# A decoder layer on one core: the down projection by seven block products, with h's operands kept in DRAM

## The chip, the core and the metric

The kernel runs on one core of one Trainium2 chip. The metric is the device time of one execution in microseconds (us), smaller is better. Of the kernel before, three runs took 2142.36, 2143.44 and 2143.82 us; the median is 2143.44 us. The profiled execution that all rows below come from took 2143.53 us, and its span, from the first to the last instruction, is 2141.7 us.

## The reference

One decoder layer works on 512 tokens of width 2048, in float32:

```python
hn   = rms_norm(x, norm_mix_pre);  proj = hn @ w_in          # 2048 -> 6144
a    = diff_attention(q, k, v, ...);  c = gate_b * short_conv(gate_c * hc, conv_w)
x    = x + rms_norm(concat(a, c) @ w_out, norm_mix_post)
hn   = rms_norm(x, norm_ffn_pre)
f    = (silu(hn @ w_gate) * (hn @ w_up)) @ w_down            # 2048 -> 5632 -> 2048
out  = x + rms_norm(f, norm_ffn_post)
```

The change is in the last two matrix stages: gate/up (two matrices of 2048 x 5632) and down (5632 x 2048). Below, h is the 512 x 5632 matrix silu(gate) * up.

## The kernel before

**Number format.** A float32 operand is split into a high part and a rest, both in TensorE's reduced float32 type: `split` (L95 to L97) has ScalarE (ACT) cast the high part (L96) and VectorE (DVE) subtract it from the source for the low part (L97). One product of two tiles is then three matmuls, high x high, high x low and low x high, issued by `mm3` (L118 to L121). So nearly all matmuls of the kernel have line L119, L120 or L121, and nearly all casts and subtractions L96 and L97.

**Gate and up.** The 5632 columns of w_gate and w_up are taken 256 at a time, gate and up by turns, as 44 *quartets* (the 2 x 2 blocks of such a piece of weights). A quartet is computed with seven block products instead of eight, by a Strassen-Winograd scheme: `combine` (L770) forms sums and differences of weight blocks on DVE, `prepare` (L784) splits the operand of one product into one of four ring tiles, `product` (L806) issues its 8 x 3 matmuls of 256 columns, and `gather` (L823) puts the products together in SBUF. Operands of the activations (`ffn_hi`, `ffn_lo` in `acts`, and the places x0 to x5) are made once, before this stage. `gate_up` (L865) issues the products in the order of the list `order` (L738) and prepares operands three products ahead. `finish` (L852) multiplies silu(gate) by up; the first 4 of h's 44 chunks of 128 rows stay in SBUF, the other 40 go to DRAM as `hd` (L863).

**Down.** 5632 is 44 chunks of 128. The chunks are taken in 5 groups of 4, 12, 12, 12 and 4 (`first_kc`, L900). For the group in work, h's chunks are read back from `hd` (`load_h`, L902), split, and kept. Weights come 4 chunks x 512 columns at a time, 1 MB, with rows of 2 KB (`down_spec`, L918), are split into two ring tiles each (`load_chunk`, L106), and used for four token tiles of 128: `down_part` (L922) issues 4 x 3 matmuls of 512 columns, with h's tile stationary and the weights moving. When a group's last chunk is in, `add_down` (L928) adds the bank to the sum in SBUF. The last group (`down_last`, L953) also adds up squares, normalizes, adds the residual read back from `x1d` and stores the result.

**What sets the order.** The program is written as jobs (`run_jobs`, L156); a tile scheduler then places instructions on each engine and adds the waits. Each engine works through its list in order; the DMAs of this part are all issued by SyncE's queue (SP), in order as well. A pool of SBUF tiles that is closed and replaced by another makes the first writers of the new tiles wait for the last users of the old ones.

Of the kernel before, what the change touches and what calls it, by code (L numbers as in the profile page):

```python
# [11 lines left out]
F32 = mybir.dt.float32  # L12
# [6 lines left out]
P = 128  # L19
# [13 lines left out]
SUB_EPS = 1e-5  # L33
LAMBDA_INIT = 0.8 - 0.6 * math.exp(-0.3 * 0)
# [19 lines left out]
def trunk(ctx: ExitStack, tc: tile.TileContext, a, out):  # L54
# [511 lines left out]
    hd = dram.tile([FF // P, P, S], F32, name="hd")  # L566


    def place(tag, dtype=F32, shape=(P, D)):
        count = late["count"] = late.get("count", 0) + 1  # L570
        name = f"{tag}_{count}"
        return late["fp"].tile(list(shape), dtype, tag=tag, bufs=1, name=name)

    def open_ffn(_):
        late["fp"] = ctx.enter_context(tc.tile_pool(name="ffn", bufs=1))
        late["mix"] = [place(f"m{t}") for t in range(NT)]
# [162 lines left out]
    raws, heads_raw, operands, psq, tmp, slots, hts = {}, {}, {}, {}, {}, {}, {}  # L739
# [44 lines left out]
    def prepare(n):  # L784

        q, i = order[n]
        if i in (1, 2) and 0 < q < HEAD:
            src = heads_raw[q][:, 8 * (i - 1) : 8 * i, :]
        else:
            (p11, p21), (p12, p22) = ((r[:, :, :P], r[:, :, P:]) for r in raws[q])  # L790
            src = {1: p11, 2: p12, 3: p12, 4: p22, 5: tmp.get("s1"), 6: p21, 7: p21}[i]
            if i in (3, 6):
                combine(q, {3: 4, 6: 2}[i])
        w = ring_tile(16, P, f"w_{q}_{i}").rearrange("p (a k) m -> p a k m", a=2)
        split(w[:, 0], w[:, 1], src)
        operands[n] = w

    def moving(i, part, k):
# [5 lines left out]
        return late[{6: 2, 7: 3, 4: 4}[i]][part].rearrange("p (t k n) -> p t k n", t=2, n=P)[:, :, k, :]  # L804

    def product(n):  # L806
        q, i = order[n]
        if i == 1:
            psq[q] = {"a": mm_bank(f"pa_{q}")}
        pq = psq[q]  # L810
        if i == 5:
            pq["b"] = aux_bank(f"pb_{q}")
        if i == 6:
            pq["d"] = (mm_bank if q else aux_bank)(f"pd_{q}")
        if i == 3:
            pq["c"] = aux_bank(f"pc_{q}")
        bank, half = {1: "a0", 2: "a1", 5: "b0", 7: "b1", 3: "c0", 4: "c1", 6: "d0"}[i]
        o = pq[bank][:, 256 * int(half) :][:, :256]
        w = operands.pop(n)
        for k in range(8):  # L820
            mm3(o, w[:, 0, k, :], w[:, 1, k, :], moving(i, 0, k), moving(i, 1, k), k == 0, k == 7)

    def gather(n):  # L823
# [3 lines left out]
        if i == (5 if early else 1):  # L827
            tmp["q1", q] = slot("q1")
            nc.scalar.copy(tmp["q1", q], pq["a"][:, :256])  # L829
            if not up:  # L830
                tmp["sg", c] = slot("sg")
            tmp["r", q] = slot("r") if up else tmp["sg", c]
        if i == 7:
# [3 lines left out]
        if i == 6:  # L837
            u = tmp["u", q] = slot("u")
            nc.vector.tensor_add(u, pq["d"][:, :256], tmp["q1", q])
            nc.vector.tensor_add(tmp["r", q][:, 768:], tmp["r", q][:, 768:], u)  # L840
        if i == (6 if early else 2):
            nc.vector.tensor_add(tmp["r", q][:, :256], pq["a"][:, 256:], tmp["q1", q])
        if i != 4:
            return
        u, r, sg = tmp["u", q], tmp["r", q], tmp["sg", c]
        nc.vector.tensor_add(r[:, 256:768], pq["c"], tmp["q57", q])
        mid = r[:, 256:768].rearrange("p (h n) -> p h n", h=2)
        nc.vector.tensor_tensor(out=mid, in0=mid, in1=u[:, None, :].broadcast_to([P, 2, 256]), op=ALU.add)
        if not up:
            nc.scalar.activation(sg, sg, AF.Silu)  # L850

    def finish(q):  # L852
# [3 lines left out]
        sg, r = tmp["sg", c], tmp["r", q]  # L856
        nc.vector.tensor_mul(sg, sg, r)
        if c < 2:
            if c == 0:
                hts[0] = [tuple(place(t, F32R, (P, 4, S)) for t in ("spare", "m3"))]  # L860
            split(*(x_[:, 2 * c : 2 * c + 2, :].rearrange("p k n -> p (k n)") for x_ in hts[0][0]), sg)
# [158 lines left out]
```

## Time and profile before

| what | value |
|---|---|
| median of three runs | 2143.44 us |
| profiled execution, its span | 2143.53 us, 2141.7 us |
| TensorE (PE) busy | 2110.2 us, 99% of the span |
| weight loads (PEld), beside PE | 1886.7 us, 88% |
| DVE busy | 1308.1 us, 61% |
| ACT busy | 809.3 us, 38% |
| gate/up, from its first product to down's first | 785.2 to 1651.7 us |
| down without the last group | 1651.7 to 2088.6 us |
| last group, norm and store | 2088.6 to 2141.7 us |

Busy shares are means over stages that differ: DVE is busy 84% of a stretch of gate/up and a third of one of down. Matmuls overlap each other, so the time between the starts of two matmuls, not the duration of one, tells what a matmul costs. "Idle before" in a group of instructions is idle time of that engine just ahead of them, and the releaser is what ended it.

### The profile page before, as it was taken

The page shows a single profiled execution, that of the slowest core. Times are in us where ns is not written, and L with a number is a line of the kernel's source. Part 1 is how long each engine was busy: PE and PEld are TensorE (multiplying, and loading weights), DVE is VectorE, ACT ScalarE, POOL GpSimd, SP SyncE. Part 2 cuts the span into 40 slices and gives each one's busy share as a digit, 9 for nine tenths or more (in the row PEclk, how much of TensorE's full clock was granted, in tenths as well). Part 3 has the DMA queues.
Part 4 walks back from the last instruction along what each step waited for, and adds up shares of the span by engine and source line. Part 5 has one row for each costly group of instructions (what it writes and reads, how often), then busy time and mean ns, then how long its engine had stood idle before and what let it go on. Part 6 is the DMA issues. An engine that isn't in the chain of part 4 may idle for free.

```text
span 2141.7 us, 30431 instructions
## 1 busy us (share of the span) xinstructions
PE 2110.2 (99%) x13118; PEld 1886.7 (88%) x13118; DVE 1308.1 (61%) x1635; ACT 809.3 (38%) x1065; POOL 30.2 (1%) x51
## 2 busy tenths in 40 slices
PE   7999999999999998999999999999999999999998
PEld 6888888888888888999999999999999888888886
DVE  5226355463752389988888888888887532422336
ACT  4234243443532265544444444444444321211122
POOL 0000000000000010000000000000000000000000
PEclk9999999999999999999999999999999999999999
DMA  7322322222234343333333343333433532423233
GB/s 246 113 99 89 99 84 86 97 89 99 79 138 137 138 171 119 125 120 128 129 125 103 128 138 128 110 119 129 138 109 133 216 125 97 157 99 118 98 118 118
DMA packets 197831, 261.74 MB, mean 122 GB/s; under 512 B 9368, under 2 KB 146584, under 8 KB 195264
## 3 DMA queue, kind: packets, MB, share of 16 engines
q1 hardware_dynamic: 196384, 255.05, 35.0%
q10 hardware_dynamic: 1312, 4.74, 0.7%
q8 instruction: 103, 1.69, 0.3%
q14 instruction: 32, 0.26, 0.0%
HBM read 240.88 MB, written 21.52 MB: 123 GB/s over the span
## 4 chain that ended last, share of the span: by engine, by line
PE 94%; DVE 4%; DMA 1%; issue 0%; ACT 0%; POOL 0%; SPq 0%; DVEq 0%; POOLq 0%; ACTq 0%
PE pd L121 9%; PE pd L120 9%; PE pd L119 9%; PE pa L119 4%; PE pc L121 3%; PE pc L119 3%; PE pc L120 3%; PE pb L121 3%; PE pb L119 3%; PE pb L120 3%; PE pa L120 3%; PE pa L121 3%; PE po L119 3%; PE po L120 3%; PE po L121 3%; PE pc_h L119 1%
## 5 line engine op out<-in xcount | busy, mean ns | idle before, releaser
L97 DVE TENSOR_TENSOR lo_d<-raw_d,hi_d 128x2048 fp32r<-128x2048 f32 x42 | 96.2, 2291 | 185.5 <-ACT hi_d L96 185.5
L119 PE MATMUL pa<-acts,w 128*128 128x256 f32 x704 | 199.1, 283 | 1.1 <-ACT w L96 0.8
L121 PE MATMUL pa<-acts,w 128*128 128x256 f32 x704 | 194.8, 277 | 0.3 <-DVE w L97 0.3
L120 PE MATMUL pa<-acts,w 128*128 128x256 f32 x704 | 195.0, 277 | 0.0
L96 ACT CAST w<-raw_q 128x1024 fp32r<-128x1024 f32 x130 | 136.5, 1051 | 134.8 <-PE pc L121 33.5
L96 ACT CAST hi_d<-raw_d 128x2048 fp32r<-128x2048 f32 x42 | 80.0, 1906 | 277.5 <-PE pd L121 262.6
L97 DVE TENSOR_TENSOR w<-raw_q,w 128x1024 fp32r<-128x1024 f32 x130 | 156.8, 1221 | 13.7 <-ACT w L96 13.7
L119 PE MATMUL pd<-hi_d,acts 128*128 128x512 f32 x384 | 149.4, 389 | 0.0
L121 PE MATMUL pd<-hi_d,acts 128*128 128x512 f32 x384 | 149.4, 389 | 0.0
L120 PE MATMUL pd<-lo_d,acts 128*128 128x512 f32 x384 | 149.4, 389 | 0.0
L119 PEld LDWEIGHTS pa<-acts,w 128*128 128x128 f32 x704 | 132.2, 188 | 9.2 <-ACT m L829 8.2
L121 PEld LDWEIGHTS pa<-acts,w 128*128 128x128 f32 x704 | 132.2, 188 | 0.5 <-DVE w L97 0.5
L120 PEld LDWEIGHTS pa<-acts,w 128*128 128x128 f32 x704 | 132.2, 188 | 0.0
L121 PE MATMUL pb<-acts,w 128*128 128x256 f32 x352 | 98.1, 279 | 3.0 <-DVE w L97 3.0
L119 PE MATMUL pd<-x,w 128*128 128x256 f32 x352 | 98.0, 278 | 1.7 <-ACT w L96 1.7
L121 PE MATMUL pd<-x,w 128*128 128x256 f32 x352 | 98.3, 279 | 1.3 <-DVE w L97 1.3
L119 PE MATMUL pb<-acts,w 128*128 128x256 f32 x352 | 97.9, 278 | 0.1
L120 PE MATMUL pd<-x,w 128*128 128x256 f32 x352 | 97.9, 278 | 0.0
L121 PE MATMUL pc<-acts,w 128*128 128x256 f32 x352 | 97.3, 276 | 0.5 <-DVE w L97 0.5
L120 PE MATMUL pb<-acts,w 128*128 128x256 f32 x352 | 97.8, 278 | 0.0
L119 PE MATMUL pc<-acts,w 128*128 128x256 f32 x352 | 97.2, 276 | 0.0
L120 PE MATMUL pc<-acts,w 128*128 128x256 f32 x352 | 97.2, 276 | 0.0
(283 smaller groups left out, 6122.6 us busy)
## 6 DMA issues: line engine op xcount, KB each, us to landing
raw_q<-in_w_gate SPq DMA_DIRECT2D x44, 1024.0 KB, 5.1
raw_d<-in_w_down SPq DMA_DIRECT2D x44, 1024.0 KB, 5.0
post<-in_w_up SPq DMA_DIRECT2D x22, 1024.0 KB, 5.1
pre<-in_w_up SPq DMA_DIRECT2D x22, 1024.0 KB, 5.4
raw_o<-in_w_out SPq DMA_DIRECT2D x16, 1024.0 KB, 5.0
hd<-m SPq DMA_DIRECT2D x20, 512.0 KB, 2.8
raw_h<-hd SPq DMA_DIRECT2D x10, 1024.0 KB, 5.1
raw_v<-in_w_in SPq DMA_DIRECT2D x8, 1024.0 KB, 6.7
```

The costliest lines, as they stand in the source:

```text
L96: nc.scalar.copy(hi, src)
L97: nc.vector.tensor_tensor(out=lo, in0=src, in1=hi.bitcast(F32), op=ALU.subtract)
L119: nc.tensor.matmul(o, lhsT=lhi, rhs=rhi, start=start, stop=False)
L120: nc.tensor.matmul(o, lhsT=lhi, rhs=rlo, start=False, stop=False)
L121: nc.tensor.matmul(o, lhsT=llo, rhs=rhi, start=False, stop=stop)
```

## The change

`quartets`, products and rings of gate/up stay. New is that

- of the 22 pieces of h (256 rows, two chunks each), 20 (`NP`) go through the down projection by seven block products: a pair of chunks x two halves of the tokens is a 2 x 2 block of h, and the pair x two halves of 512 columns is a 2 x 2 block of w_down. The last two pieces (4 chunks) go as before, in `down_last`;
- `finish` makes the four sums and differences of h's blocks on DVE, and the high and low parts of all seven operands; `store_h` writes them to DRAM (`hx`, 7 operands x 20 pairs, high and low; `hl` for the last 4 chunks);
- the 20 pairs are taken in three groups of 7, 7 and 6 (`FIRST`). `load_slot` reads one operand of a group, high and low, both token halves, in four DMAs, into the place of gate/up's (or the former group's) operand of the same product, as soon as that product has been computed for the last time;
- weights come as blocks of 7 (or 6) chunks x 256 columns, 1 KB rows (`load_block`); DVE forms the four differences; each product is done in two halves of 4 and 3 (or 3 and 3) pairs, called steps: 3 groups x 4 column blocks x 7 products x 2 halves = 168 steps, each with 24 or 18 matmuls of 256 columns;
- products that enter the same sums are accumulated in one bank, in down and in gate/up too: there, product 2 is added to product 1's half bank, 3 and 4 to those of 5 and 7 (fewer adds on DVE, one more copy on ACT);
- the sums `late["f"]` are a new tile in a new pool, opened where the pool `mids` (the places m0 to m3) is closed;
- the first products of the first four quartets are issued in another order.

```diff
-    order = [(q, i) for q in range(HEAD) for i in (1, 2)]
-    order += [(q, i) for q in range(2 * NC) for i in ((5, 7, 6, 3, 4) if q < HEAD else (1, 2, 5, 7, 6, 3, 4))]
+    order = [(q, i) for p in (0, 2) for i in (1, 2) for q in (p, p + 1)]
+    order += [(q, i) for q in range(2 * NC) for i in ((5, 7, 6, 3, 4) if q < HEAD else (1, 5, 7, 2, 6, 3, 4))]
...
     def finish(q):
...
-        nc.vector.tensor_mul(sg, sg, r)
-        if c < 2:
...
-            nc.sync.dma_start(hd[2 * c : 2 * c + 2].rearrange("j p n -> p j n"), sg.rearrange("p (j n) -> p j n", j=2))
+        h = place("m3", F32R)
+        f = h.bitcast(F32)
+        nc.vector.tensor_mul(f[:, :1024], tmp["sg", c], tmp["r", q])
+        if c < NP:
+            b = [f[:, 256 * i : 256 * i + 256] for i in range(7)]
+            nc.vector.tensor_add(b[4], b[1], b[3])
+            nc.vector.tensor_sub(b[1], b[0], b[1])
+            nc.vector.tensor_sub(b[5], b[3], b[1])
+            nc.vector.tensor_sub(b[6], b[2], b[5])
+        n = 1792 if c < NP else 1024
+        hi = place("spare" if c < NC - 1 else "pre", F32R)
+        nc.scalar.copy(hi[:, :n], f[:, :n])
+        tmp["h", c] = h, hi, n
+    def store_h(q):
...
+        nc.vector.tensor_tensor(out=h[:, :n], in0=h.bitcast(F32)[:, :n], in1=hi.bitcast(F32)[:, :n], op=ALU.subtract)
+        for part, x_ in enumerate((hi, h)):
+            if c < NP:
+                nc.sync.dma_start(
+                    hx[part, :, c, :, :, :].rearrange("p b t n -> p (b t n)"), x_[:, :n].bitcast(F32)
...
+    FIRST = (0, 7, 14, NP)
+    HALVES = ((0, 4), (4, 7))
+    steps = [(g, cb, i, hf) for g in range(3) for cb in range(4) for i in (1, 5, 7, 2, 6, 3, 4) for hf in range(2)]
...
+    def load_slot(i, g):
...
+        v = slots_d[i] = slot_view(i, g)
+        for part in range(2):
+            for t in range(2):
+                nc.sync.dma_start(v[part][t].bitcast(F32), hx[part, :, FIRST[g] : FIRST[g + 1], BLOCK[i], t, :])
+    def prepare_down(n):
...
+        if i == 5:
+            nc.vector.tensor_sub(b11, b12, b11)
+        if i == 7:
+            nc.vector.tensor_sub(b12, b22, b12)
+        if i == 6:
+            nc.vector.tensor_sub(b11, b22, b11)
+        if i == 4:
+            nc.vector.tensor_sub(b21, b21, b11)
...
+        w = ring_tile(2 * len(ks), 256, f"w_d{n}").rearrange("p (a k) m -> p a k m", a=2)
+        split(w[:, 0], w[:, 1], src)
...
+    def product_down(n):
...
+        for t in range(2):
+            o = bank[:, t * 256 : (t + 1) * 256]
+            for j, k in enumerate(ks):
+                mm3(
+                    o, xh[t][:, k, :], xl[t][:, k, :], w[:, 0, j, :], w[:, 1, j, :],
...
+    def gather_down(n):
...
+        if "f" not in late:
+            mids.close()
+            late["sums"] = ctx.enter_context(tc.tile_pool(name="sums", bufs=1))
+            late["f"] = late["sums"].tile([P, NT, D], F32, name="f")
...
+        if i == 1:
+            tmp["qd"] = late["sums"].tile([P, 512], F32, tag="qd", bufs=1, name=f"qd_{s}")
+            nc.scalar.copy(tmp["qd"], pd[s, 1])
+        u = two(tmp["qd"])
+        if i == 5:
+            onto(f22, bank(5), g == 0)
+        if i == 7:
+            onto(f22, bank(7))
+        if i == 2:
+            onto(f11, bank(1), g == 0)
+        if i == 6:
+            nc.vector.tensor_add(u, u, bank(6))
+            onto(f22, u)
+        if i in (3, 4):
+            f, b = (f12, bank(5)) if i == 3 else (f21, bank(7))
+            if g == 0:
+                nc.vector.tensor_add(f, b, u)
+            else:
+                onto(f, b)
+                onto(f, u)
+    def ffn(_):
...
+            if i == 6 and q > 0:
+                store_h(q - 1)
+            if q == last_q:
+                load_slot(i, 0)
         finish(last_q)
+        store_h(last_q)
+        load_block(1, 0)
```

**Where instructions stand now.** In these rows `w_dN` is the ring tile of step N, `pd_s_i` the bank of product i in column block s (0 to 11 over the three groups), `qd` the copy of product 1, `f` the sums. First ACT, at the end of gate/up. Before, the casts of down's weights follow those of the last quartet:

```order
L835 COPY m2_29_5995<-pb_43_14830 128x512 [waits PE_49]
L96 CAST hi_d0_0_0_14942<-raw_d0_0_0_14940 128x2048 [waits DMAHW4_49,Activation_49]
L96 CAST hi_d0_1_0_14976<-raw_d0_1_0_14974 128x2048 [waits DMAHW5_49,DVE_49,PE_49]
L96 CAST acts_72<-raw_h4_14995 128x2048 [waits DMAHW7_49]
L96 CAST acts_72<-raw_h8_15044 128x2048 [waits DMAHW0_49]
L96 CAST hi_d0_2_0_15050<-raw_d0_2_0_15048 128x2048 [waits DMAHW2_49,DVE_49,PE_49]
```

Now, after the casts of steps 8, 9, 12 and 13:

```order
L98 CAST w_d8_15252<-spare_123_14750 128x1024 [waits DVE_49,PE_49]
L98 CAST w_d9_15280<-spare_123_14750 128x768 [waits DVE_49,PE_49,Activation_49]
L98 CAST w_d12_15356<-post_126_14976 128x1024 [waits DVE_49,PE_49]
L98 CAST w_d13_15384<-post_126_14976 128x768 [waits DVE_49,PE_49]
L1048 COPY qd_0_15145<-pd_0_1_15093 128x512 [waits DMAHW6_49,DMAHW5_49,DMAHW4_49]
L1041 COPY f_15144<-pd_0_5_15151 128x2x256
L98 CAST w_d10_15302<-raw_b0_2_14754 128x1024 [waits PE_49]
L1041 COPY f_15144<-pd_0_1_15093 128x2x256 [waits PE_49]
L98 CAST w_d11_15330<-raw_b0_2_14754 128x768
L98 CAST w_d14_15410<-pre_133_15091 128x1024 [waits DMAHW6_49,DVE_49,PE_49]
```

The copy `qd_0`, the first writer in the new pool, waits for three DMAs, and all later casts stand behind it. On PE the products of the first column block are in the order 1, 5, 7, 6, 2, 3, 4.

Second SP's queue at the same place. Before:

```order
L955 DMA pre_90_17332<-in_norm_ffn_post 128x2048 [waits DMAHW6_49,DMAHW2_49,DVE_49]
L908 DMA raw_h4_14995<-hd_551 128x4x512 [waits DMAHW4_49,DVE_49]
L908 DMA raw_h8_15044<-hd_551 128x4x512 [waits DMAHW5_49,DVE_49]
L863 DMA hd_551<-m0_28_5962 128x2x512 [waits DMAHW1_49,DVE_49]
L109 DMA raw_d0_2_0_15048<-in_w_down 128x4x512 [waits DMAHW7_49,DVE_49]
```

Now, the end of a run of 28 such loads of h's operands:

```order
L977 DMA acts_72<-hx_551 128x7x128 [waits DMAHW6_49]
L977 DMA x4_129_15078<-hx_551 128x7x128 [waits DMAHW7_49,PE_49]
L977 DMA x4_129_15078<-hx_551 128x7x128 [waits DMAHW0_49]
L977 DMA x5_130_15079<-hx_551 128x7x128 [waits DMAHW1_49]
L977 DMA x5_130_15079<-hx_551 128x7x128 [waits DMAHW2_49]
L914 DMA hl_552<-pre_132_15086 128x1024 [waits DMAHW3_49,Activation_49]
L914 DMA hl_552<-m3_131_15084 128x1024 [waits DMAHW4_49,DVE_49]
L944 DMA raw_b1_1_15180<-in_w_down 128x7x256 [waits DMAHW5_49,DVE_49]
```

The DMAs of the queue take the semaphores DMAHW0 to DMAHW7 by turns; the store of m3_131, the last DMA that uses a tile of the pool `mids`, has DMAHW4, and it stands behind all 28 loads.

Third DVE, in steady work in down. Before, per four token tiles: three subtractions of 2048 columns and four adds:

```order
L97 TENSOR_TENSOR lo_d3_1_1_16807<-raw_d3_1_1_16804,hi_d3_1_1_16806 128x2048 [waits DMAHW2_49,Activation_49]
L97 TENSOR_TENSOR lo_d3_1_2_16865<-raw_d3_1_2_16862,hi_d3_1_2_16864 128x2048 [waits DMAHW3_49,Activation_49]
L97 TENSOR_TENSOR lo_d3_2_0_16919<-raw_d3_2_0_16916,hi_d3_2_0_16918 128x2048 [waits DMAHW4_49,Activation_49]
L935 TENSOR_TENSOR m0_74_14993<-m0_74_14993,pd_3_1_0_16810 128x512 [waits PE_49]
L935 TENSOR_TENSOR m1_75_15012<-m1_75_15012,pd_3_1_1_16823 128x512 [waits PE_49]
```

Now, where one column block ends and the operands of the next are made:

```order
L1043 TENSOR_TENSOR f_15144<-f_15144,pd_4_5_16645 128x2x256 [waits PE_49]
L987 TENSOR_TENSOR post_145_16508<-raw_b5_1_16674,post_145_16508 128x1024 [waits DMAHW2_49,DVE_49]
L1043 TENSOR_TENSOR f_15144<-f_15144,qd_4_16639 128x2x256 [waits DVE_49]
L99 TENSOR_TENSOR w_d71_16932<-post_145_16508,w_d71_16932 128x768 [waits Activation_49]
L989 TENSOR_TENSOR raw_b5_1_16674<-raw_b5_2_16827,raw_b5_1_16674 128x1024 [waits DMAHW4_49,DVE_49]
L99 TENSOR_TENSOR w_d72_16956<-post_145_16508,w_d72_16956 128x1024 [waits Activation_49]
L1043 TENSOR_TENSOR f_15144<-f_15144,pd_4_7_16698 128x2x256 [waits PE_49]
```

Each step of a product now has a subtraction of its own on DVE (L99), most have a difference of weight blocks before it (L987 to L993), and the adds of the sums stand in between.

## Rows read from the trace of the kernel before

**Rows 1.** What PE waited for: engine, line, releaser, us in total, times, longest

```profile
PE pt_pre L128 <- DVE xn L138: 9.4, 1, 9.4
PE pb L121 <- DVE w L97: 3.0, 1, 3.0
```

**Rows 2.** Windows: length; busy us of PE, PEld, DVE, ACT, POOL; PEclk, DMA share, GB/s

```profile
800.00:805.00 5.00, 5.00 (x45) 5.00 (x45) 5.00 (x7) 4.44 (x8) 0.00 (x0) 1.00 1.07 329
...
1000.00:1200.00 200.00, 199.93 (x1735) 197.96 (x1734) 167.70 (x182) 90.54 (x99) 0.00 (x0) 1.00 0.38 127
...
1700.00:1750.00 50.00, 50.00 (x222) 41.42 (x221) 17.23 (x11) 11.45 (x6) 0.00 (x0) 1.00 0.50 186
```

**Rows 3.** Timeline of PE in gate/up: start us, duration us; 18 matmuls apart

```profile
1600.08 0.28 PE L119 MATMUL pb<-acts,w 128*128 128x256 f32 x1
...
1602.12 0.28 PE L119 MATMUL pb<-x,w 128*128 128x256 f32 x1
```

**Rows 4.** Line L119 by operand, down stage: count, durations ns, first and last start

```profile
L119 PE MATMUL pd<-hi_d,spare x64: 388/388/390, 1651.7 to 1694.9; 128*128 128x512 f32 x64
...
L119 PE MATMUL pd_l<-hi_d,x x32: 392/394/398, 2088.6 to 2131.9; 128*128 128x512 f32 x32
```

**Rows 5.** DVE groups by shape: busy us, mean ns of one | idle before, releaser

```profile
L97 DVE TENSOR_TENSOR w<-raw_q,w 128x1024 fp32r<-128x1024 f32 x130 | 156.8, 1221 | 13.7 <-ACT w L96 13.7
L97 DVE TENSOR_TENSOR lo_d<-raw_d,hi_d 128x2048 fp32r<-128x2048 f32 x42 | 96.2, 2291 | 185.5 <-ACT hi_d L96 185.5
...
L848 DVE TENSOR_TENSOR m<-m,m 128x512 f32<-128x512 f32 x44 | 30.2, 686 | 0.0
...
L836 DVE TENSOR_TENSOR m<-m 128x256 f32<-128x256 f32 x44 | 18.7, 426 | 25.6 <-ACT m L835 25.6
```

**Rows 6.** ACT groups by shape, as rows 5

```profile
L96 ACT CAST w<-raw_q 128x1024 fp32r<-128x1024 f32 x130 | 136.5, 1051 | 134.8 <-PE pc L121 33.5 <-DVE raw_q L780 32.3 <-DVE raw_q L782 25.9
...
L835 ACT COPY m<-pb 128x512 f32<-128x512 f32 x44 | 25.8, 586 | 64.6 <-PE pb L121 64.4
```

**Rows 7.** DMA issues of 1 MB: us from issue to landing

```profile
raw_d<-in_w_down SPq DMA_DIRECT2D x44, 1024.0 KB, 5.0
...
DMA to landing us min/median/max: 7.7/9.0/10.3
```

**Rows 8.** SP's issues beside the next rows: start us; L768 reads 512-byte rows

```profile
641.38 0.38 SPq L109 DMA_DIRECT2D raw_o<-in_w_out  x1
641.81 0.50 SPq L638 DMA_DIRECT2D x<-in_x  x1
642.36 0.43 SPq L768 DMA_DIRECT2D spare<-in_w_up  x1
...
787.97 0.38 SPq L768 DMA_DIRECT2D post<-in_w_gate  x1
...
794.68 0.38 SPq L768 DMA_DIRECT2D spare<-in_w_up  x1
```

**Rows 9.** Windows of 1 us, columns as rows 2

```profile
650.00:651.00 1.00, 1.00 (x6) 0.81 (x5) 0.52 (x1) 0.44 (x1) 0.00 (x0) 1.00 1.20 289
...
791.00:792.00 1.00, 1.00 (x11) 1.00 (x10) 1.00 (x2) 0.45 (x1) 0.00 (x0) 1.00 1.17 329
796.00:797.00 1.00, 1.00 (x12) 1.00 (x11) 1.00 (x3) 0.45 (x1) 0.00 (x0) 1.00 1.03 221
831.00:832.00 1.00, 1.00 (x11) 1.00 (x11) 1.00 (x2) 0.00 (x0) 0.00 (x0) 1.00 1.05 357
1673.00:1674.00 1.00, 1.00 (x6) 0.84 (x5) 1.00 (x1) 0.00 (x0) 0.00 (x0) 1.00 1.06 414
```

**Rows 10.** Windows around a stop of PE, columns as rows 2

```profile
822.00:824.00 2.00, 0.39 (x4) 0.20 (x2) 2.00 (x2) 2.00 (x3) 0.00 (x0) 1.00 0.00 0
...
826.00:828.00 2.00, 2.00 (x11) 2.00 (x11) 2.00 (x4) 1.05 (x1) 0.00 (x0) 0.50 0.19 30
828.00:830.00 2.00, 2.00 (x16) 2.00 (x16) 1.31 (x2) 0.00 (x0) 0.00 (x0) 0.82 1.02 340
```

More of the change, by code (lines that the diff above doesn't have):

```diff
@@ new lines, in slot_view @@
+    def slot_view(i, g):
+        n = FIRST[g + 1] - FIRST[g]
+        if i in (1, 2, 3, 5):
+            t0, k0 = (0 if i < 3 else 2), (8 if i in (2, 3) else 0)
+            return [
+                [acts[:, o + 32 + (t0 + t) * D + k0 * P :][:, : n * P].rearrange("p (k n) -> p k n", n=P) for t in range(2)]
+                for o in (0, 128 + NT * KC * P)
+            ]
+        if ("slot", i, g) not in late:
+            x0 = {6: 0, 7: 2, 4: 4}[i]
+            late["slot", i, g] = [place(f"x{x0 + part}", F32R) for part in range(2)]
+        return [
+            [x_[:, 32 + t * 1024 :][:, : n * P].rearrange("p (k n) -> p k n", n=P) for t in range(2)]
+            for x_ in late["slot", i, g]
+        ]
@@ new lines, in prepare_down @@
+    def prepare_down(n):
+        if n >= len(steps):
+            return
+        g, cb, i, hf = steps[n]
+        s = 4 * g + cb
+        ks = pairs(g, hf)
+        b11, b12, b22, b21 = (blocks[s, j][:, ks.start : ks.stop, :] if (s, j) in blocks else None for j in range(4))
+        if i == 5:
[4 more added lines that the diff above has]
+            nc.vector.tensor_sub(b11, b22, b11)
+        if i == 4:
+            nc.vector.tensor_sub(b21, b21, b11)
+        src = {1: b11, 5: b11, 7: b12, 2: b21, 6: b11, 3: b22, 4: b21}[i]
+        w = ring_tile(2 * len(ks), 256, f"w_d{n}").rearrange("p (a k) m -> p a k m", a=2)
+        split(w[:, 0], w[:, 1], src)
+        operands_d[n] = w
+        if hf == 1:
+            if i == 7:
+                load_block(s + 1, 1)
+            if i == 3:
+                load_block(s + 1, 2)
+            if i == 4:
+                load_block(s + 1, 3)
+                load_block(s + 2, 0)
@@ new lines, in product_down @@
+    def product_down(n):
+        g, cb, i, hf = steps[n]
+        s = 4 * g + cb
+        ks = pairs(g, hf)
+        if hf == 0 and i in (1, 5, 7, 6):
+            pd[s, i] = (mm_bank if i in (1, 6) else aux_bank)(f"pd_{s}_{i}")
+        bank = pd[s, {1: 1, 2: 1, 5: 5, 3: 5, 7: 7, 4: 7, 6: 6}[i]]
+        w = operands_d.pop(n)
+        xh, xl = slots_d[i]
+        for t in range(2):
+            o = bank[:, t * 256 : (t + 1) * 256]
+            for j, k in enumerate(ks):
+                mm3(
+                    o, xh[t][:, k, :], xl[t][:, k, :], w[:, 0, j, :], w[:, 1, j, :],
+                    i in (1, 5, 7, 6) and hf == 0 and t == 0 and j == 0, hf == 1 and t == 1 and j == len(ks) - 1, True,
+                )
@@ L953, in down_last @@
-    def down_last(ch):
-        gfin = place("pre")
-        nc.sync.dma_start(gfin, a["norm_ffn_post"][0:1, :].broadcast_to([P, D]))
+        store_h(last_q)
+        load_block(1, 0)
+        for n, (g, cb, i, hf) in enumerate(steps):
+            product_down(n)
+            yield
+            gather_down(n)
+            while ready < min(ng + n + 4, ng + len(steps)):
+                prepare(ready)
+                ready += 1
+            if cb == 3 and hf == 1:
+                load_slot(i, g + 1)
+            if g == 2 and cb == 3:
+                tail_loads(i, hf)
@@ L956, in down_last @@
+    def down_last(_):
         for t in range(NT):
-            xt = place("spare" if t % 2 else "m3")
+            xt = place(f"x{4 + t % 2}")
             nc.sync.dma_start(xt, x1d[t])
```

242 lines of the change are left out of this document (140 added, 102 removed).

## The prediction

> **What bounds the kernel now.** I read PE's waits first [rows 1]: the longest is 9.4 us, at the start of the program, and none is longer than 3.0 us after it; none lies in down. Then the windows by stage [rows 2]: PE is busy all 200 us of a stretch of gate/up and all 50 us of one of down. So from 830 us to the last group nothing but the number and the pace of matmuls sets the time. DVE is the next engine: 167.7 of 200 us in gate/up, 17.2 of 50 in down. It can work with no gap: 5.00 of 5.00 us in the window at 800 [rows 2]. The change takes matmul time out of down and puts work on DVE and on the DMA queue there. What counts is whether both keep up.
>
> **Matmuls in down.** Before, the 40 chunks cost 40 x 4 token tiles x 4 column groups x 3 = 1920 matmuls of 512 columns, from 1651.7 us to the first of the last group at 2088.6 [rows 4]: 436.9 us, 0.2276 each. After, 20 pairs x 7 products x 2 token tiles x 4 column blocks x 3 = 3360 matmuls of 256 columns. Such a matmul, with new weights each time, is gate/up's own form: 18 of them start within 2.04 us [rows 3], 0.1133 each. 3360 x 0.1133 = 380.8 us. The term is -56.1 us if PE never stops; halving the width costs nothing here, since a matmul of 256 takes half of one of 512.
>
> **DVE in down.** A subtraction of 1024 columns takes 1.22 us and an operation of 512 takes 0.69 [rows 5]; 768 columns, between the two, 0.95. A column block with 7 pairs has 7 splits and 4 differences, each of 1024 + 768 columns: 11 x 2.17 = 23.9 us; and 9 adds of 512 in the second group: 6.2; together 30.1, beside 294 matmuls x 0.1133 = 33.3 us. In the first group there are 5 adds: 27.3. In the third, with 6 pairs, 22 operations of 768 and 9 adds: 27.1 us beside 28.6. So DVE has room of 10% in the second group and 5% in the third, and PE's operands are made three steps ahead (over 6 us). From below the cost is nothing. From above: DVE waits for ACT's cast before every second split; a cast of 768 is about 0.9 us (1.05 for 1024, [rows 6]), so 6.3 us a block: 3.1 x 4 + 4.8 x 4 = 32 us. In gate/up those waits were 13.7 us over 130 splits [rows 5], 0.1 each, which would be 1.5 us a block and leave almost nothing. That row is the nearest; I take 3 us.
>
> **gate/up.** DVE per two quartets was 167.7 / 200 x 38.1 = 31.9 us [rows 2] (2 x 168 matmuls x 0.1133 = 38.1). Off go, twice, an add of 512 and one of 256 (2.2 us); on come four adds of 256 (1.7, [rows 5]) and one split of 1792 columns, 2.0 us between the rows for 1024 and 2048: 33.4 us, 88%, still covered by PE. If it were not covered it would be 1.5 us x 22 = 33 us; since DVE had no gap at all at 800 us and PE went on, I take nothing. ACT gets a cast of 1792 and has more than half its time free. The new order of the first products lies where PE stood for single waits of at most 3.0 us [rows 1]: 0, give or take 3.
>
> **The passage from gate/up to down.** This is a new wait. Call the start of the last quartet T. After each of its products, SP issues that product's `load_slot`: 128 x 7 x 128 x 4 bytes x 4 loads = 1.835 MB, in pieces of 512 bytes. Nothing before read so much so fast. The nearest rows are the single loads of 512-byte rows by L768 [rows 8]: when they alone were moving, all DMA engines busy, 289 and 329 GB/s [rows 9]; 221 with a store beside them (796 us); 1 KB rows 357, down's own 2 KB rows (1673 us) 414. I take 309: 5.9 us per operand, against 2.7 us in which PE does a product. So a backlog builds from the first load on.
>
> Behind the 28 loads, in the same queue, stands the store of the last piece of h out of m3; and ACT's copy `qd_0`, first writer in the pool that replaces m0 to m3, waits for it. That DMAs of the queue land in the order of issue is seen at 642 us: the third of three loads issued within 1 us [rows 8] took 10.3 us [rows 7]. Landing of the store: T + 2.7 (first product done) + 7 x 5.94 = 41.6 + one weight block of 0.92 MB at 357 GB/s 2.6 + the two stores of 0.52 MB at some 400, 2.6 + 2.4 from transfer to landing (1 MB lands in 5.0 us [rows 7], of which 2.6 are transfer) = T + 51.9; with the copy, 0.6 [rows 6], T + 52.5.
>
> PE has by then the quartet (168 x 0.1133 = 19.0 us) and, in its new order, products 1, 5, 7 and 6 of the first block, 4 x 42 x 0.1133 = 19.0: T + 38.1. Product 2 is added onto the bank that `qd_0` copies, and 3 and 4 need casts that stand behind it on ACT. So PE stands 14.4 us. Bounds: at 329 GB/s 11.9, at 221 30.9. After a stop of some us the granted clock is half (0.50 at 826, 0.82 at 828 [rows 10]) and comes back: half of 2 us and a fifth of 2, 1.4; I take 1.7, for a longer stop. Together +16.1 us.
>
> The Trainium skill ("DMA: Bandwidth & Descriptors", Specifications) gives 512 bytes as the smallest transfer that runs at line rate; the rows above speak against it, 289 and 329 where 2 KB rows reach 414. By the rule, 512-byte pieces would move like the 2 KB rows; that is the second rival below.
>
> **The two changes of group.** S is the start of a group's last column block, 33.3 us long. Loads start at S + 4.8; with them go four weight blocks of 2.6. The last operand is there at S + 4.8 + 41.6 + 10.4 + 2.4 = S + 59.2 and wanted at S + 33.3 + 6 x 4.76 = S + 61.9. Into the third group 6-pair operands (5.1 us each) and smaller blocks: S + 4.8 + 35.6 + 8.8 + 2.4 = S + 51.6, wanted at 57.8. No stop, but the first has 2.7 us to spare, and one weight block behind five operands comes only just in time: 1 us.
>
> **The rest.** The last group's 192 matmuls and the end after them stay (53.1 us, 2088.6 to 2141.7).
>
> **Sum**, against the profiled execution's 2143.5 us (the median of the runs is the same to 0.1): 2143.5 - 56.1 + 16.1 + 3 + 1 = **2107.5 us**.
>
> **Rivals.**
>
> 1. *The reads are too slow.* Reads of 512 bytes for 42 us, at places 7 KB apart, with writes and 1 KB reads between, may run nearer to the 221 GB/s of 796 us. With u us per operand the stop at the passage is 7u - 27.2, at the first change of group 7u - 44.3, at the second 6u - 41.8: at u = 8.3 that is 30.9 + 13.8 + 8.0, with three clock losses 5.1 and the 4 us above 61.8: 2149 us, slower than before. It decides from u = 8.0, 229 GB/s, on. For it: that one window. Against: the two windows without a store; only 1 MB of stores lies in this run of reads. 12%, of which 4 within 0.2%.
> 2. *512-byte pieces run like 2 KB rows* (414 GB/s, u = 4.4): the stop is 3.6 us and 1.7 for the clock: 2143.5 - 56.1 + 5.3 + 4 = 2097 us. For it the rule, against it rows 9. 12%.
> 3. *DVE sets the pace of down.* A cast waited for at every third split or so in the third group and at the changes of group, half of the upper bound above: 16 us, in place of 3: 2121 us. For it: 27.1 us of work in 28.6; the differences bunch where one block follows another. Against: waits of 0.1 us in gate/up. 14%.
> 4. *The copy does not wait for the store* (the wait stands for an earlier DMA, or the store overtakes the loads): then operands of products come at most some 3 us late: 2143.5 - 56.1 + 3 + 4 = 2094 us. Against it the 10.3 us of the third load. 8%.
>
> **How the numbers follow.** The forecast has 54%, with its own range from 2101 (329 GB/s, no loss to DVE or at the changes) to 2121 (262 GB/s: u = 7.0, stops of 21.8, 4.7 and 0.2, two clock losses, and the 4 us). What a measurement can tell from no change is 0.2%, 4.3 us. Rivals 2, 3 and 4 and the forecast all end below 2139: faster 0.88; rival 1 gives 0.04 for the same and 0.08 for slower. The range that is to hold 8 times in 10 goes from 2093, which keeps most of rivals 2 and 4, to 2128, which keeps most of rival 3 and leaves out rival 1.
>
> **What the changed profile would show.** Right: PE starts 256-column matmuls of down 0.1133 us apart; one gap of 12 to 16 us some 38 to 41 us after the last quartet's start, ended by ACT's copy of `pd`, which a DMA of m3 to `hl` released; the DMA share near or over 1 for 45 us from that quartet on, at some 300 GB/s; DVE 90 to 95% busy in the last two groups, with PE gaps of tenths of a us. Wrong: gaps of PE at every column block, ended by DVE (rival 3); gaps at the changes of group ended by loads of `hx` (rival 1); no gap of over 6 us at the passage (2 or 4); or PE waits in gate/up, which I cost at nothing.

## The result and the profile after

The changed kernel takes 2125.99 us (median of 14 runs) against 2143.65 us before (14 runs beside them): a ratio of 0.9911, with a 95% interval from 0.9883 to 0.9939. A ratio, here and below, leaves out the runs that are over 1.5% longer than the fastest of their kernel, here the two of 2141.7 us. The changed kernel is faster, as forecast, and its median is inside the range (2093 to 2128), but 18.5 us above the forecast of 2107.5. The median hides something: the 14 runs of before lie between 2142.36 and 2145.41, those of after between 2108.29 and 2141.73. Three microseconds of spread have become 33, and 6 of the 14 runs lie above the range.

The profiled run is one of the quick ones, 2111.91 us with a span of 2109.8. What PE waited for in it (engine, line, releaser, us in total, times, longest), beside [rows 1]:

```profile
PE pd L123 <- ACT qd L1048: 13.6, 1, 13.6
PE pt_pre L132 <- DVE xn L142: 9.5, 1, 9.5
PE pd L124 <- DVE w_d L99: 5.2, 5, 2.5
...
PE pa L123 <- DMA acts<-hx: 2.5, 1, 2.5
```

The first line is the stop at the passage: one wait, ended by ACT's copy `qd`, 13.6 us for a forecast of 14.4. Asked for the tile `qd` in this stretch, the profile names what ACT waited for, and who for ACT:

```profile
L1048 ACT COPY qd<-pd x1: 585/585/585, 1683.1 to 1683.1; 128x512 f32<-128x512 f32 x1
...
  DMA hl<-m: 12.1, 1
...
  PE pd L123: 13.6, 1
```

It is the store of m3 to `hl`, as forecast. SP's issues (start us, us of the issue, destination <- source, count) show the queue in front of it:

```profile
1627.93 10.33 SPq L977 DMA_DIRECT2D acts<-hx  x8
...
1667.46 6.30 SPq L977 DMA_DIRECT2D x<-hx  x4
1673.87 1.45 SPq L914 DMA_DIRECT2D hl<-pre  x1
1675.42 0.38 SPq L914 DMA_DIRECT2D hl<-m  x1
```

The windows of the passage (columns as [rows 2]) give the rate, to be held against [rows 9], and the clock after the stop, against [rows 10]:

```profile
1650.00:1660.00 10.00, 10.00 (x87) 10.00 (x87) 9.84 (x11) 4.73 (x5) 0.00 (x0) 1.00 1.08 284
1660.00:1670.00 10.00, 9.84 (x84) 9.56 (x83) 6.29 (x7) 3.77 (x4) 0.00 (x0) 1.00 1.10 286
1670.00:1680.00 10.00, 0.13 (x2) 0.00 (x0) 1.39 (x2) 0.83 (x1) 0.00 (x0) 0.76 1.14 304
1680.00:1690.00 10.00, 6.30 (x34) 6.30 (x35) 1.98 (x3) 1.97 (x3) 0.00 (x0) 0.56 0.96 266
```

From 284 to 304 GB/s with all DMA engines busy, where 309 was taken; so an operand takes some 6.3 us, and the store was seen by ACT at T + 58 (T, the start of the last quartet, is 1625.1) instead of T + 51.9. PE got there late too, at T + 44.8 instead of T + 38.1, and the two errors cancel. The clock cost 2.5 us, not 1.7: 34 matmuls, 3.9 us at the full clock, took 6.3 us at 0.56.

The budget of this run, in spans (2141.7 to 2109.8): gate/up's last quartet starts 7.2 us earlier, for which I had 0; that quartet, up to down's first matmul, takes 5.5 more; down with its stops saves 30.9; the last group and the end take 0.7 more. Sum -31.9.

### The profile page after: what moved, and what is told of

It reads as the page before. It is cut to its first block, busy times and chain, and to the rows that moved or that the text cites. A ratio compares the mean times of both kernels' runs of the same rounds, so it can differ in the third digit from the quotient of the medians.

```text
span 2109.8 us, 34073 instructions
## 1 busy us (share of the span) xinstructions
PE 2053.5 (97%) x14558; PEld 1912.1 (91%) x14558; DVE 1492.9 (71%) x1893; ACT 909.9 (43%) x1263; POOL 30.1 (1%) x51
## 4 chain that ended last, share of the span: by engine, by line
PE 70%; DVE 16%; DMA 9%; issue 2%; ACT 1%; SPq 0%; POOL 0%; DVEq 0%; POOLq 0%; ACTq 0%
DVE w L99 6%; PE pd L124 5%; PE pd L125 5%; PE pd L123 5%; DMA raw_q<-in_w_gate 4%; PE pb L125 3%; PE pb L123 3%; PE pb L124 3%; DMA pre<-in_w_up 3%; PE po L123 3%; PE po L124 3%; PE po L125 3%; PE pa L125 2%; PE pa L124 2%; PE pa L123 2%
## 5 line engine op out<-in xcount | busy, mean ns | idle before, releaser
L123 PE MATMUL pb<-acts,w 128*128 128x256 f32 x704 | 195.7, 278 | 2.2 <-ACT w L98 2.2
L125 PE MATMUL pb<-acts,w 128*128 128x256 f32 x704 | 195.5, 278 | 1.8 <-DVE w L99 1.8
L125 PE MATMUL pb<-x,w 128*128 128x256 f32 x704 | 194.9, 277 | 1.3 <-DVE w L99 1.3
L124 PE MATMUL pb<-acts,w 128*128 128x256 f32 x704 | 195.4, 278 | 0.0
L124 PE MATMUL pb<-x,w 128*128 128x256 f32 x704 | 194.6, 276 | 0.0
L123 PE MATMUL pb<-x,w 128*128 128x256 f32 x704 | 194.5, 276 | 0.0
L123 PE MATMUL pd<-w_d,acts 128*128 128x256 f32 x640 | 178.9, 279 | 13.6 <-ACT qd L1048 13.6
L124 PE MATMUL pd<-w_d,acts 128*128 128x256 f32 x640 | 179.3, 280 | 5.1 <-DVE w_d L99 5.0
L125 PE MATMUL pd<-w_d,acts 128*128 128x256 f32 x640 | 178.6, 279 | 0.0
L99 DVE TENSOR_TENSOR w<-raw_q,w 128x1024 fp32r<-128x1024 f32 x130 | 158.6, 1220 | 4.9 <-ACT w L98 4.8
L123 PEld LDWEIGHTS pb<-acts,w 128*128 128x128 f32 x704 | 133.2, 189 | 2.6 <-ACT w L98 2.6
L125 PEld LDWEIGHTS pb<-acts,w 128*128 128x128 f32 x704 | 133.0, 189 | 2.0 <-DVE w L99 2.0
L123 PEld LDWEIGHTS pd<-w_d,acts 128*128 128x128 f32 x640 | 122.0, 191 | 13.8 <-ACT qd L1048 13.8
L125 PEld LDWEIGHTS pb<-x,w 128*128 128x128 f32 x704 | 132.2, 188 | 1.9 <-DVE w L99 1.9
L124 PEld LDWEIGHTS pb<-acts,w 128*128 128x128 f32 x704 | 133.1, 189 | 0.0
```

Of the source, the lines that this page charges most:

```text
L99: nc.vector.tensor_tensor(out=lo, in0=src, in1=hi.bitcast(F32), op=ALU.subtract)
```

## The experiments

**The changed kernel once more (again).** No edit; the question was what differs between two of its runs.

> The changed kernel once more, for a second profile, since its 14 runs lie between 2108 and 2142 us. If the reads of hx set the difference, a longer run shows a lower GB/s in the 45 us of the passage (291 in the first profile) and longer PE gaps there and at the two changes of group, about 20 us more time for each 1.0 us more per operand read (6.3 us in the first profile). If DVE sets it, the gaps of PE lie at all column blocks and the GB/s stays.

2119.99 us. The stop at the passage is the same, 13.8 us, and so are the DMA rates. What differs is a stretch of down in which PE waits in neither run. PE alone in this run (window, its length, busy us and matmuls, clock, DMA share, GB/s):

```profile
1000.00:1600.00 600.00, 598.62 (x5272) 1.00 0.47 159
1700.00:1800.00 100.00, 100.00 (x852) 1.00 0.51 143
```

and in the first profile of the same kernel:

```profile
1000.00:1600.00 600.00, 598.91 (x5273) 1.00 0.47 159
1700.00:1800.00 100.00, 100.00 (x885) 1.00 0.56 154
```

In gate/up both do 5272 or 5273 matmuls in 600 us. In down one does 885 in 100 us, the other 852, at a full clock in both and busy all the time. So matmuls of 256 columns have two steady paces: 113.3 ns from start to start, or 117.8 ns. The slow one held here from 1693 to 2056 us, 363 us, and cost 363 x 0.0377 = 13.7 us (0.0377 is 1 - 5097 / 5297, by the counts of a slow and a quick stretch further down); the first profile's longer gaps at the changes of group give some of it back, and 8.1 us are left between the runs. The idea that the DMA rate varies has no support in these rows. For all that follows: 851 or 852 in 100 us is slow, 884 or 885 quick; 5097 in 600 us is slow, 5297 quick.

**The order of the products alone, in the kernel before (e4).**

```diff
-... for i in ((5, 7, 6, 3, 4) if q < HEAD else (1, 2, 5, 7, 6, 3, 4))]
+... for i in ((5, 7, 6, 3, 4) if q < HEAD else (1, 5, 7, 2, 6, 3, 4))]
-            if i in (3, 6):
-                combine(q, {3: 4, 6: 2}[i])
+            if i in (3, 6) or (i == 7 and q >= HEAD):
+                combine(q, {3: 4, 6: 2, 7: 3}[i])
-            elif q >= HEAD and i == 1:
-                combine(q, 3)
```

> The kernel before with gate/up's products issued in the changed kernel's order (1, 5, 7, 2, 6, 3, 4) and nothing else. In the first profile of the changed kernel a quartet takes 19.12 us, before 19.33; the weight loads of product 2 waited 8.2 us in all for ACT's copy of product 1 (L829). Theory (that wait is what gate/up gained): 40 quartets x 0.2 us, 8 us less, 2135.5 us. Rival (the gain came from the fewer adds on DVE): no change, 2143.5 us.

2132.5 us (median of five runs), ratio 0.996 (0.9948 to 0.9973): by the median -11 us, where -8 was expected. So gate/up's gain is the order. Before, product 2 went into the bank that ACT was copying product 1 out of; the copy's line in the kernel before says who waited for it:

```profile
L829 ACT COPY m<-pa x44: 372/372/378, 824.1 to 1635.2; 128x256 f32<-128x256 f32 x44
...
  PEld pa L119: 8.2, 40
```

These are 40 stops of 0.2 us, which PE's waits in [rows 1] do not list, since the weight load (PEld) carries them. From start to start such a stop costs 0.28 us (around 1035.6 us, two gaps of 284 and 221 ns where 113 is usual), and 40 of them make the 11 us. I had costed the new order at 0. Without the stops the five runs lie between 2132.1 and 2138.81 us: a spread of 7 us, where the 12 runs of before beside them have 0.8, but far from 33.

**The last chunk's stores ahead of three operands (e1).**

```diff
-            if q == last_q:
+            if q == last_q and i in (1, 5, 7, 2):
                 load_slot(i, 0)
         finish(last_q)
         store_h(last_q)
+        for i in (6, 3, 4):
+            load_slot(i, 0)
```

> Only the order in SP's queue differs: h's last store stands after four of the seven operand reads, not after all. Theory (the stop of 13.6 us at the passage is the store waiting behind the reads): the store lands some 35 us after the last quartet's start instead of 58, the copy qd is there before PE wants it, and what is left are waits of about 3 us for the last two operands: 10 us of stop and about 3 of clock less, 2097 to 2100 us in a run like the profiled one (2111.9), 13 less than the changed kernel in the mean. Rival (reads of hx themselves hold PE, the store only happens to land then): the stop moves to the next operand and the time stays within 4 us.

2129.07 us (2121.01 to 2137.21), ratio 0.9934: no gain over the changed kernel. Taken alone, it would have refuted the theory of the passage. The profile (2127.97 us) shows otherwise. The longest waits of PE from 1640 to 1730 us:

```profile
PE pa L123 <- DMA acts<-hx: 1.4, 1, 1.4
PE pa L124 <- DMA acts<-hx: 1.1, 1, 1.1
PE pd L125 <- DMA x<-hx: 1.0, 1, 1.0
```

The stop for `qd` is gone. But all of gate/up ran at the slow pace:

```profile
1000.00:1600.00 600.00, 600.00 (x5097) 1.00 0.45 152
1740.00:1800.00 60.00, 60.00 (x532) 1.00 0.51 145
```

It lasted from 834 to 1661 us and cost 828 x 0.0377 = 31.2 us. Without it this run would be at 2096.8, where 2097 to 2100 was expected. So by this estimate the stop is worth its length and its clock, and the slow pace hid that; none of the six runs shows it by its time.

**Operands laid out for the reads (e3).** `hx` is stored so that a read takes 3.5 KB in one piece, and a write 512 bytes.

```diff
-    hx = dram.tile([2, P, NP, 7, 2, P], F32, name="hx")
+    hx = dram.tile([2, P, 7, 2, NP, P], F32, name="hx")
```

> Only the layout of hx in DRAM differs: one operand's pairs are contiguous, so a read moves pieces of 3584 (3072) bytes instead of 512, and the stores, spread over gate/up, pieces of 512. Theory (pieces of 512 bytes make the reads slow): 400 GB/s instead of 291 in the passage, 4.5 us per operand instead of 6.3, the stop 13.6 us becomes 1 to 2, the waits of 3.6 us in the last quartet 1, those at the change of group none: about 2090 us, and if slow reads make the runs differ, a spread of a few us instead of 33. Rival (the rate is the memory's, whatever the pieces): time and spread stay. Second rival: the stores in small pieces hold up gate/up's weights: PE waits for raw_q or post there, time up.

2092.48 us (2086.86 to 2117.68), ratio 0.978 (0.9743 to 0.9817). At the passage, PE's wait and the windows:

```profile
PE pd L123 <- ACT qd L1048: 4.2, 1, 4.2
```

```profile
1625.00:1650.00 25.00, 23.31 (x201) 22.94 (x200) 18.73 (x21) 9.97 (x12) 0.00 (x0) 1.00 1.02 381
1650.00:1660.00 10.00, 9.84 (x85) 9.63 (x84) 7.83 (x8) 3.77 (x4) 0.00 (x0) 1.00 1.02 400
```

381 and 400 GB/s where pieces of 512 bytes reached 284 to 304: the layout set the rate, and the rate the stop. (With the size of the pieces their distance changed too; the two were not tried apart.) The writes in 512-byte pieces landed in 9.4 us instead of 8.8, which nothing waits for. The Trainium skill ("DMA: Bandwidth & Descriptors", Specifications) has 512 bytes as the least size for line rate; the trace does not agree, neither here nor in [rows 9].

**The stop back in every quartet of the changed kernel (e5).** If the missing stops let a slow pace last, putting them back should narrow the spread.

```diff
-... else (1, 5, 7, 2, 6, 3, 4))]
+... else (1, 2, 5, 7, 6, 3, 4))]
```

> The changed kernel with the products of a gate or up quartet in the old order (1, 2, 5, 7, 6, 3, 4), all else as it is: product 2 goes into the bank that ScalarE copies product 1 out of, so TensorE stops there for about 0.28 us once per quartet, 40 times, as it did in the kernel before. Theory of the two pitches: matmuls of 256 columns that run without a stop go at one of two steady pitches, 113.3 or 117.8 ns, drawn at a stop and kept until the next; with a stop in every quartet the slow pitch lasts 19 us at most instead of 800. Gate/up then costs its 8 us more than in the quick run of the changed kernel and no more in any run; down (3,360 matmuls x 4.4 ns = 15 us) is still drawn. So 2116 to 2133, median about 2121, no run above 2136, though the kernel has more stops than the changed one. Rival: the 33 us between runs come from the DMA of the passage or of the operands; then the spread stays, 2116 to 2150, median about 2134.

2139.16 us, seven runs from 2136.42 to 2142.72: the spread fell to 6 us, as the theory says, but the level is 6 us above its range. The stops were longer than in the kernel before:

```profile
PE pa L123 <- ACT m L853: 11.4, 18, 0.7
```

In every second quartet ACT was at another operation, and the stop came to 0.9 us from start to start. The passage and the change of group were longer too (16.3 and 5.3 us). So this kernel supports the theory by its spread alone.

**The stop in every fourth quartet only (e19).** The same edit for `q % 4 == 0`, ten short stops.

> The changed kernel with the old order of the products (1, 2, 5, ...) in every fourth quartet only: ten stops of 0.28 us in gate/up, and all else as it is. e5 had the stop in every quartet, and in the up quartets it came to 0.9 us, because ScalarE was at another operation; the ten quartets here are gate quartets, where e5's stop was 0.28 us. Theory of the two pitches: 2 to 3 us more than the quick run of the changed kernel (2108 to 2112), and up to 10 us where down is slow: 2110 to 2126, no run above 2128, so the median is below the changed kernel's 2126 although the kernel has ten stops more. Rival (the spread has another cause, and e5's was narrow since its longer stops hid it): 2110 to 2145, median about 2128.

2114.64 to 2123.86 us (4 runs), median 2122.11. On this chip the kernel before took 2152.48, which gives a ratio of 0.9853 (0.9831 to 0.9874). Median and spread (9 us) are as the theory says. That ten more stops make the changed kernel faster is not shown: the two medians are 4 us apart, inside the changed kernel's spread, and the ratios come from different chips. Its profile, cut at the stops of 1264.9, 1344.4 and 1420.8 us:

```profile
1190.00:1264.00 74.00, 74.00 (x655) 1.00 0.48 164
1266.00:1340.00 74.00, 74.00 (x630) 1.00 0.48 164
1346.00:1420.00 74.00, 74.00 (x655) 1.00 0.47 165
1422.00:1496.00 74.00, 74.00 (x631) 1.00 0.48 164
```

Quick, slow, quick, slow: the pace changes at a stop and is kept until the next one. This is the clearest sight of it. The kernel before had 40 such stops, so the one slow draw in its profile lasted 20 us; without stops one can last 800.

**Layout and store order together (e13)**: the edits of e1 and e3.

> The layout of e3 (operand reads in 3.5 KB pieces, writes in 512 B pieces) and the order of e1 (the last chunk's stores ahead of the last three slots). Theory: e3's profile still had a stop of 4.2 us for qd and a half clock of 3.4 us after it; with the stores earlier both go, so 2079 to 2084 where both pitches are the quick ones; a run whose gate/up goes at the slow pitch is 30 us longer (2109 to 2114), one whose down does is up to 15 us longer. Rival (the stores are not what the stop waits for, or SP's issues of the reads set the pace): as e3, 2087 at best.

2080.93, then 2094.57, 2095.34, 2095.93, then 2118.94 and 2124.93 us; the ratio is 0.9751 (0.9726 to 0.9776). Three groups, 14 us and then 23 us or more apart. The quick one is the 2079 to 2084 of the expectation. Only the middle one has a profile:

```profile
1000.00:1600.00 600.00, 600.00 (x5296) 1.00 0.52 162
1700.00:1800.00 100.00, 100.00 (x852) 1.00 0.69 231
```

Down was slow from its first matmul (1642.5) to its last: 397 x 0.0377 = 15.0 us. PE had no wait between 1632 and 2029 us, so here the pace changed without a stop, at the change from gate/up's operands to down's.

**The two, with stops in every fourth quartet (e14).**

> e13 with the old order of the products (1, 2, 5, ...) in every fourth quartet only, so a stop of about 0.2 us at ten places of gate/up. Theory of the two pitches: 2 us more than e13's quick runs and no run whose gate/up stays slow for more than a quarter of 300 us: 2081 to 2086 in most runs, at most 2101 (down slow), spread half of e13's or less. Rival (the spread has another cause): the spread is that of e13 and e3, some 30 us.

2097.39 to 2103.39 us (4 runs). In its profile gate/up is quick (5276 matmuls in 600 us), down slow again (852 in 100 us). So the level is that of a slow down, and only the spread came as expected: 6 us, where e13 had 44.

**A stop in down (e15).** ACT reads one column of product 1's bank between its halves, in six column blocks.

```diff
+        if i == 1 and hf == 1 and cb % 2 == 0:
+            nc.scalar.copy(small.tile([P, 1], F32, tag="peek", name=f"peek_{s}"), bank[:, 511:512])
```

> e14 with, in every second column block of down (six in all), a one-column read of product 1's bank by ScalarE between its two halves, so that TensorE's second half has to wait for it. In e13 and e14 down switched to 117.8 ns with its very first matmul, for lack of any stop, and kept it for 390 us. Theory of the two pitches: each short stop draws the pitch anew, nearly always the quick one, so down costs 15 us less and the stops some 0.5 us each (ScalarE may be at a split): 2083 to 2089, all runs within 8 us. Rival (down's pitch is not drawn at stops, or the stop is filled with other matmuls and doesn't come about): as e14, 2097 to 2103.

2098.81 to 2102.91 us: by its time, the rival's result. By its profile neither:

```profile
1000.00:1600.00 600.00, 599.93 (x5184) 1.00 0.50 157
1700.00:1790.00 90.00, 90.00 (x794) 1.00 0.54 169
```

Down is quick now (794 in 90 us), but not because of the reads: its first 24 matmuls, from 1662.78 to 1665.40 us, are quick already, and the first read stops PE only behind them, at 1665.9 us. And gate/up, where nothing was edited, is at neither pace. Start times of PE at one change of operand, 24 matmuls each:

```profile
1203.34 0.28 PE L123 MATMUL pa<-x,w 128*128 128x256 f32 x1
...
1206.05 0.28 PE L125 MATMUL pa<-x,w 128*128 128x256 f32 x1
1206.17 0.28 PE L123 MATMUL pb<-acts,w 128*128 128x256 f32 x1
...
1208.78 0.28 PE L125 MATMUL pb<-acts,w 128*128 128x256 f32 x1
```

23 steps take 2.71 us with the moving operand in an x tile and 2.61 with it in `acts`. By the program, the new tile stands in a pool that comes before the x tiles, and moves them by a few bytes; `acts` lies in a pool on the other side.

**The same reads without a new tile (e16).** The column goes into a tile that is there already (`tag="ss1"`).

> e15 with the six one-column reads put into a tile that is there already (tag ss1) instead of a new one, so that no other tile moves. In e15 the new tile (4 buffers of 4 bytes a partition) came into a pool that lies under the tiles x0 to x5, and in gate/up the products whose moving operand is in an x tile ran at 117.6 to 117.8 ns, those out of acts at 113.3 to 113.8. Theory: the place of the moving operand in SBUF decides which pitch follows at a change of operands, a short stop gives back the quick one; so here gate/up is quick throughout as in e14, down is quick behind its first read as in e15: 2084 to 2090, all runs within 8 us. Rival (the reads themselves disturb gate/up, or each program has its own pitch whatever the tiles): gate/up mixed as in e15, 2098 to 2103.

2093.06 to 2104.13 us, on a chip where the kernel before took 2155.43: ratio 0.9741 (0.9726 to 0.9756). It is the lowest ratio of all, against a slower kernel before; by time e3's and e13's medians (2092.48 and 2095.64) are below its 2097.65. Gate/up by pieces of four quartets:

```profile
1192.00:1268.00 76.00, 76.00 (x648) 1.00 0.51 160
1269.00:1345.00 76.00, 76.00 (x671) 1.00 0.51 160
...
1499.00:1575.00 76.00, 76.00 (x647) 1.00 0.51 160
```

The mixture by operand is gone; slow and quick change at the stops, as in e19. Two of the ten stretches between stops drew the slow pace, 3 us each. In down this profile does show what a read does: the matmuls ahead of the first read (1653.28 to 1656.34 us) are 117.7 ns apart, those behind it 113.3. The times are above the 2084 to 2090 expected, on a chip that is slower for the kernel before too, and the spread is 11 us, not 8. Its interval overlaps that of e13's quicker runs; what e16 has ahead of e13 and e3 is that none of its five runs falls back by 20 us or more.

**The new tile alone**, zeroed once: in the changed kernel (e17), and in e14, whose gate/up was quick (e18).

```diff
+    nc.vector.memset(small.tile([P, 1], F32, tag="pad", name="pad"), 0.0)
```

> The changed kernel with one more tile of 4 bytes a partition (4 buffers) in the pool under the x tiles, set to zero once at the start, and nothing else. Theory that the tiles' place decides: gate/up goes product by product at 113.3 (acts) and 117.8 ns (x), a mean of about 115.4, in every run alike: 14 us above the changed kernel's quick runs in gate/up, and the spread of gate/up is gone; 2122 to 2140. Rival (the place has nothing to do with it): 2108 to 2142 as the changed kernel, pitch of gate/up steady through all its products.

2124.11 to 2142.26 us, ratio 0.9909, and gate/up slow with all operands (5096 in 600 us): not the mixture but one pace, as the rival has it, so the theory's forecast failed here.

> e14 with the pad tile of e17 (4 bytes a partition, 4 buffers, under the x tiles) and no reads. e14's gate/up was quick in every run; e15, which had the reads and the shift, was mixed by operand (acts 113.7, x 117.6). Theory that the shift alone does that: gate/up mixed here too, 13 us longer than e14: 2108 to 2118, gate/up's mean pitch 115.4. Rival (e15's mixture had nothing to do with the shift; e17 was slow by a draw): gate/up quick, 2097 to 2104 (with a slow down), or 2082 to 2086 with a quick one.

2097.92 to 2106.92 us, ratio 0.9763, and the mixture is back, almost to a matmul:

```profile
1000.00:1600.00 600.00, 599.93 (x5182) 1.00 0.50 158
```

5182 for e15's 5184. e14 (5276) differs by the tile alone, and e19, on the same chip as this run, has the stops without the tile and no mixture. So four bytes more per partition in each of a pool's buffers, never used again, change the pace of the matmuls that read tiles behind them, in the two profiles that have the tile and the stops. Why e17, which has no stops, stayed slow for `acts` as well is open.

The times are 10 us below the 2108 to 2118 expected, because down is quick from its first step on:

```profile
1700.00:1800.00 100.00, 100.00 (x885) 1.00 0.61 195
```

It has no read and no wait before 2035 us, so quick or slow in down needs no stop to be decided. What goes with it is the pace just before. The last 24 matmuls of gate/up and 24 of down's first 48, in e14:

```profile
1642.48 0.28 PE L123 MATMUL pb<-x,w 128*128 128x256 f32 x1
...
1645.09 0.28 PE L125 MATMUL pb<-x,w 128*128 128x256 f32 x1
1645.20 0.28 PE L123 MATMUL pd<-w_d,acts 128*128 128x256 f32 x1
...
1647.91 0.28 PE L125 MATMUL pd<-w_d,acts 128*128 128x256 f32 x1
```

and here:

```profile
1658.54 0.28 PE L123 MATMUL pb<-x,w 128*128 128x256 f32 x1
...
1661.25 0.28 PE L125 MATMUL pb<-x,w 128*128 128x256 f32 x1
...
1664.10 0.28 PE L123 MATMUL pd<-w_d,acts 128*128 128x256 f32 x1
...
1666.71 0.28 PE L125 MATMUL pd<-w_d,acts 128*128 128x256 f32 x1
```

In e14 23 steps take 2.61 us and then 2.71, here 2.71 and then 2.61. All 12 profiles of kernels with the new down stage agree: quick turns into slow at this change in eight (after, again, e1, e3, e13, e14, e16, e19), slow into quick in four (e5, e15, e17, e18). In six of the eight a stop at the passage, or in e16 the first read, then ended the slow start; e13 and e14 have no such stop and kept it. By this pattern their slow down was no draw. That is read from the traces: no kernel was built to test it, and what e13's run of 2080.93 us did there is not known.

## Why the prediction was right, and where it was not

The forecast was faster, and the kernel is. The mechanism was right at the place on which the prediction spent most words. That the median, 2126, fell inside the range is luck: its upper part stood for rival 3, and what took the time there is a cause that the prediction does not have. **The passage** came as forecast: one stop, ended by the copy `qd`, which waited for the store of m3 behind 28 loads. Its length was right by two errors that cancel. The first is the rate (284 to 304 GB/s, not 309). The second is a wait that I missed: the operands of products 1 and 5 are loaded into `acts` while product 2 of the last quartet is to read other parts of it, and the first two matmuls of product 2 wait for the loads, 2.5 and 1.1 us in the profile; the granted clock behind them is 0.50 for 3 us. The quartet takes 24.8 us where 19.0 was reckoned, and in the quick run these 5.8 us are the largest loss that is not in the sum. The clock after the stop cost 2.5 us for 1.7.

**Matmuls in down**: 3360 x 0.1133 is what the quick runs show (885 in 100 us). The step that failed is "0.1133 each" as a constant. It was read from one stretch of one profile [rows 3]; the other pace, 117.8 ns, makes the term 15 us larger, and gate/up up to 31 us longer (e1). Of the 18 us between forecast and median, 4 are in the quick profiled run. The other 14 are, as far as is known, the pace: it is the one difference of that size that the two profiles of this kernel show (13.7 us), but the longer runs have no profile. The profile of before did show it, in one of its quartets:

```profile
1036.50:1054.50 18.00, 18.00 (x161) 1.00 0.44 147
1056.00:1074.00 18.00, 18.00 (x155) 1.00 0.36 118
1076.00:1094.00 18.00, 18.00 (x161) 1.00 0.44 147
```

155 matmuls between neighbours of 161. I read windows of 200 us, where it does not show, and did not ask what the bank wait did besides costing time.

**gate/up** at 0 was wrong by 7 us in the profiled run and 11 in e4: the wait that the new order removed stood with the weight loads, and I had looked at PE's waits alone.

**DVE in down** at 3 us: PE waits for DVE at the first change of group and right behind it, where DVE itself waits for a weight block, and once near the end; so the term is nearly 0 and rival 3 fell. **The changes of group** at 1 us were too low. Behind the operands' reads a weight block comes late, DVE waits 5.8 us for it, and PE stands:

```profile
1808.41 0.58 PE L124 MATMUL pd<-w_d,acts 128*128 128x256 f32 x1 [2.52 <-DVE w_d L99]
```

With the clock and two gaps behind it, some 6 us. "Comes only just in time" was the right sentence with the wrong price. Rivals 1, 2 and 4 fell with the 284 to 304 GB/s and the 13.6 us; rival 2 came true in e3, where the pieces were made larger.

## What to carry to other kernels

Before you call a wait on the critical path pure loss, ask what it resets: here 40 short stops, 11 us in all, each gave the pace a new draw; without them a slow pace lasted up to 800 us and cost up to 31, in some runs and not in others. Compare matmuls per window between runs, stretch by stretch, before you explain a time by DMAs or waits; and look at weight loads' waits beside PE's. When data go through DRAM, lay them out for the side that is waited for.

## What the runs showed of the hardware

- Matmuls of 256 columns, each with new weights, run at 113.3 or 117.8 ns from start to start, both with PE busy and the granted clock at 1.00. The pace is kept for as long as 800 us. It changes at stops: one slow stretch behind the 40 stops of before's profile, two behind the ten of e19's, two behind those of e16's. It is reversed at the change from gate/up to down, in all 12 profiles. It goes with the place of the moving operand in SBUF (e15, e18). What decides it at a stop was not found, and why the operands matter was not found either. Gate/up of e1 and e17 was slow in their profiles, that of the changed kernel quick in both of its own, though e1's gate/up is the same.
- In the last two sets of runs the kernel before took 2155.43 and 2152.48 us instead of 2143.5 to 2143.8, on other chips. More slow draws at its stops could do it (0.75 us a quartet), but that is a guess: no profile of it was taken there.
- Loads in pieces of 512 bytes moved 284 to 304 GB/s in a long run, 381 to 400 in pieces of 3.5 KB (after, e3).
